# A decoder trunk with paged stick-breaking attention: where the sums of output-weight quarters are made, and where the convolution's first block and the lead pieces stand

## The chip, the core and the metric

The kernel runs on one NeuronCore of a Trainium2 chip, in one launch. Its engines are TensorE (PE, with its weight loads PEld), VectorE (DVE), ScalarE (ACT), GpSimd (POOL) and SyncE (SP); each works through its own row of instructions in order, and they meet through semaphores. Here SP issues nearly all plain DMA transfers, POOL the indirect ones (gathers). The metric is the device time of one execution in microseconds (us); smaller is better.

## The reference, cut to what matters

One decoder layer (`D_MODEL` 1024, mixer width 2048) runs for a prompt of 2048 tokens and for a sample group of 8 sequences with 4 tokens each and 8192 cached tokens in pages of 128:

```
h = rms_norm(x, pre_g)
z = h @ w_in                                   # 5632 columns, split into groups
A: u = a * sigmoid(b); causal depthwise conv, width 31; layer_norm; silu; @ w_pw + b_pw
B: causal means over windows of 2, 4, 8, 16, minus the token; per-group linear; scale
C: stick-breaking attention, 8 heads of 64:
   z = q.k/8 + bias;  a = exp(log_sigmoid(z) + sum over later keys of log_sigmoid(-z));  y = a @ v
D: cross-attention, 4 heads of 128, into 256 memory tokens
mix = concat(yA*silu(gA), yB*silu(gB), yC*silu(gC), yD*silu(gD))
y = x + rms_norm(mix @ w_out, post_g);  then a final rms_norm
```

The sample group's attention reads keys and values through a page table. All is fp32; the outputs are both groups' `y`, the new keys and values, the convolution and pooling states, and the prompt's memory keys and values.

## The kernel before, in words

**Projection.** `main` (L1927) runs `z_groups`, which multiply the normalised tokens by `w_in`. Each fp32 operand is split into a high part, rounded to the fast fp32r type, and a low part (a subtraction on DVE or POOL), and three matmuls take the place of one. Beside them live `tasks`: generators, of which each gets one step per step of `main` (later statistics, bias rows, convolution and pooling of finished columns). In the same loop the sample group's attention is fed in: POOL gathers pages of keys (`kt`, 128x2048, 1 MB) and of values (`vt`, 128x1024, 512 KB; both L957), DVE transposes the keys (`T`, L990), PE makes scores (`sSA`, L1003) and the weighted values (`sO`, L1042). The gathers are issued when the buffers that they fill come free, that is when DVE has transposed the keys before (`kt`) or PE has used the values before (`vt`).

**Prompt attention.** `sb_prompt` walks over four pairs of heads `hp` (called laps below), in each over four blocks of 512 queries `qb`, and in each over the key blocks `kc` from `qb` down to 0, with four score steps for each (`q2` 0 and 2, `hh` 0 and 1). Names like `be1_2_0_1_0` carry `hp`, `qb`, `kc`, `hh`, `q2`. One step is a chain over the engines: PE scores `S` (L1297, L1298), ACT sigmoids `gam` and `be` (L1302, L1303), a DVE scan `E` (L1372, L1375), a POOL product `be*E` (L1384), PE transposes `AT` (L1403), an ACT copy `at` (L1405), PE values `av` (L1415). At the end of a block DVE multiplies `av` by the gate rows `sgt` (L1419), in place, SP stores the result to `mixd` (L1420), and the next block's `sgt` is loaded (L1436) into the same single buffer. PE's row is laid out by hand, several steps deep; for the other engines a scheduler sets the order from the program and the pools' buffers, except where the program ties an instruction to another (`issue_after`, `keep_in_program_order`).

**Side work.** From the ninth step on, every time that 4.0 us of cost have gathered (`PACE`), the attention takes one step of `side_work` (L1990): the end of the sample group (`sample_end`), then `weight_sums`, then the first output weights (`out_weights(1)`: a load, an ACT cast `wohi` and a POOL subtraction `wolo`, eight times), then, once the block (3, 0) of the last lap is flagged, four *lead* pieces of `mix` (load `mr` L1731, ACT cast `mh` L1756, POOL subtraction), and after the flag (3, 1) three more loads and the start of the convolution's last part, `conv_post`, up to its flag `"centered"`. That start is: load two blocks of 256 tokens (`cy0`, `cy256`); add the four channel tiles of the first on POOL (`total`, `cs`, L1483); multiply by ones on PE for the mean (`center`, `cm0`, L1488); subtract on DVE; squares on ACT (`csq`, L1497); three additions of squares on POOL (L1499). The column sums of the second block (`cs256`) reuse the buffer of the first.

**Output.** `mix @ w_out` is done with seven products of quarter matrices instead of eight. Products 4 to 7 multiply *sums* of weight quarters with sums of mix quarters; products 1 to 3 use quarters as they are (`FACTORS`). `SUMS` names the place of each weight sum in the DRAM buffer `wsd`; `weight_load` reads it from there during the output stage. `weight_sums` (L1613) makes them in eight rounds: two loads of 512 KB each into SBUF (`ws`, L1620), four POOL operations on 128x512 (L1627), each tied behind the newest `be*E` product, and two stores of 512 KB to `wsd` (L1630). The mix sums are combined in `out_combine` (L1736) and the products' results in `out_ready` (L1773), with signs that belong to the signs of the weight sums.

Line numbers here and in the profile are those of the kernel before. In the changed kernel the attention's lines stand four further on (L1384 is L1388, L1420 is L1424, L1483 is L1487).

Of the kernel before, what the change touches and what calls it, by code (L numbers as in the profile page):

```python
# [18 lines left out]
P = 128  # L19
# [46 lines left out]
SUM = 3  # L66
BEB = 5
# [25 lines left out]
def kernel(  # L93
# [777 lines left out]

    def sample_setup(sm, S):
# [738 lines left out]
    SUMS = {4: (0, 0), 7: (0, 1), 6: (1, 0), 5: (1, 1)}  # L1611

    def weight_sums(wsp):  # L1613

        ts = {}
        for j in range(9):
            if j < 8:
                ts[j] = [wsp.tile([P, 2, 512], F32, tag="ws", name=f"ws{j}_{n}", bufs=6) for n in range(2)]
                for t, r in zip(ts[j], half_rows(j)[::-1]):
                    sp.dma_start(t.rearrange("p b n -> p (b n)"), w_out0[r])  # L1620
            yield
            if j:
                t, u = ts.pop(j - 1)
                for o, a, b, op_ in ((t[:, 1], t[:, 1], u[:, 1], ALU.subtract), (u[:, 1], u[:, 1], u[:, 0], ALU.subtract),
                                     (u[:, 0], t[:, 1], u[:, 0], ALU.add), (t[:, 0], t[:, 0], u[:, 0], ALU.subtract)):
                    with tc.issue_after(newest[-1]):
                        pool.tensor_tensor(out=o, in0=a, in1=b, op=op_)  # L1627
                    yield
                for n, o in enumerate((t, u)):
                    sp.dma_start(wsd[n, j - 1], o)  # L1630
                yield
# [104 lines left out]
    def out_combine(x):  # L1736
        prod, i, h = x
        store()
        ts = raws[x]
        if prod == 5 and i < LAST:  # L1740
            dve.tensor_tensor(out=ts[1], in0=ts[0], in1=ts[1], op=ALU.add)
            ts = ts[1:]
        elif prod == 7:
            pool.tensor_tensor(out=ts[0], in0=ts[0], in1=ts[1], op=ALU.subtract)
            stores.append(((0, i, h), msd[0, i, h], ts[0]))
        elif prod == 6:
            tc.keep_in_program_order(dve.tensor_tensor(out=ts[0], in0=ts[0], in1=ts[1], op=ALU.subtract))
# [25 lines left out]
    def out_ready(prod, i, o):  # L1773

        if i == LAST:
# [12 lines left out]
            else:  # L1788
                dve.tensor_tensor(out=o[:NS], in0=both[:NS], in1=keep["s"][:NS], op=ALU.add)
# [11 lines left out]
        elif prod == 6:  # L1801
            dve.tensor_tensor(out=U3[:, i], in0=o, in1=U3[:, i], op=ALU.add)
            dve.tensor_tensor(out=U2[:, i], in0=o, in1=U2[:, i], op=ALU.add)
# [5 lines left out]
        else:  # L1809
# [9 lines left out]
            dve.tensor_tensor(out=c, in0=o, in1=(U2 if prod == 3 else U3)[:, i], op=ALU.add)  # L1819
# [106 lines left out]

    def main():  # L1927
        yield from z_groups(0, GROUPS[0][4:12])
        tasks.add(later_stats())
        tasks.add(bias_rows())  # L1930
# [59 lines left out]
    def side_work():  # L1990
# [6 lines left out]
        yield from out_weights(1, opm, pool)  # L1997
        while (3, 0) not in flags:
# [15 lines left out]
        while "centered" not in flags:  # L2014
            next(conv)
            yield

# [195 lines left out]
```

## Time and profile before

| what | value |
|---|---|
| median of 3 runs | 2319.89 us (2316.73 to 2320.56) |
| the profiled execution | 2319.3 us, its span 2317.6 us |
| granted TensorE clock, mean over the span | 0.993 |
| busy: PE, PEld, DVE, ACT, POOL | 97%, 78%, 74%, 47%, 54% of the span |
| projection and sample group | 60 to 1465 us |
| prompt attention with side work | 1465 to 1902.4 us |
| output projection | 1902.4 to 2317.6 us |
| POOL operations of the weight sums (L1627) | 32, from 1550.0 to 1763 us |
| DMA | 558.32 MB, mean 241 GB/s |

How to read it: the profile is one execution, and all its times are microseconds from the start of the span. A busy share is an average over the stages, so what matters is read by stage: a window gives the busy time of each engine in a stretch, its granted PE clock (1.00 is full), the busy share of the 16 DMA engines and the rate. In a timeline a row gives start, length, engine, line, operation, and in brackets how long the engine stood idle before it and what it waited for. "SPq" is SP's row of DMA issues; a DMA's own time isn't in it.

### The profile page before, as it was taken

How to read it: one execution, taken by the hardware profiler on the slowest of the kernel's cores; microseconds unless marked ns; L12 is line 12 of the kernel's file. 1: busy time of each engine (PE TensorE's matmuls, PEld its weight loads, DVE VectorE, ACT ScalarE, POOL GpSimd, SP SyncE). 2: the span in 40 equal slices, each digit the busy share in tenths (PEclk: the TensorE clock that was granted, in tenths of full speed). 3: DMA queues.
4: the chain of work that ended last, by engine and by line, in shares of the span. 5: the costliest groups of instructions: out<-in, count | busy, mean ns of one | idle time of the engine just before them, and what ended most of it. 6: DMA issues, size and time to landing. Idle time of an engine off the chain costs nothing. (4 is left out here: it accounts for less than half of the span.)

```text
span 2317.6 us, 43407 instructions
## 1 busy us (share of the span) xinstructions
PE 2244.9 (97%) x16512; PEld 1812.9 (78%) x16512; DVE 1704.7 (74%) x2334; ACT 1081.0 (47%) x1977; POOL 1261.0 (54%) x1375
## 2 busy tenths in 40 slices
PE   7999999999999999999999999999999999999997
PEld 7998888898888777777777777667677667788775
DVE  5343786969756755378777768899989885686997
ACT  5332343242442322234233234588879875454553
POOL 3554545556464555555545455489999973620002
PEclk9999999999999999999999999999999999999999
DMA  6689977878778899987977885666554307876774
GB/s 206 208 291 316 336 259 255 286 256 277 255 252 301 306 358 338 345 284 255 319 260 259 278 275 178 160 173 192 160 161 129 98 15 217 285 236 194 251 261 152
DMA packets 338188, 558.32 MB, mean 241 GB/s; under 512 B 29162, under 2 KB 213610, under 8 KB 321580
## 3 DMA queue, kind: packets, MB, share of 16 engines
q1 hardware_dynamic: 282604, 286.83, 39.9%
q0 software_dynamic: 55376, 268.72, 32.8%
q8 instruction: 130, 2.13, 0.4%
q14 instruction: 78, 0.64, 0.1%
HBM read 465.35 MB, written 90.72 MB: 240 GB/s over the span
## 5 line engine op out<-in xcount | busy, mean ns | idle before, releaser
L990 DVE STREAM_TRANSPOSE T<-kt 128x1024 f32<-128x1024 f32 x256 | 308.6, 1226 | 183.1 <-PE sSA L1003 174.8
L957 POOL DMA_INDIRECT vt<-in_cache_v_dram,idv x256 | 252.7, 987 | 255.1 <-PE sO L1042 194.2
L642 DVE SCALAR_TENSOR_TENSOR cacc<-U,par,cacc 128x512 f32<-128x512 f32 x480 | 359.9, 750 | 11.0
L1384 POOL TENSOR_TENSOR be<-be,E 128x512 f32<-128x512 f32 (+4 forms) x316 | 311.9, 999 | 18.0 <-DVE E L1375 12.4
L957 POOL DMA_INDIRECT kt<-in_cache_k_dram,idk x128 | 128.7, 1005 | 200.2 <-DVE T L990 156.0
L1375 DVE TENSOR_TENSOR_SCAN E<-gam,cr,ZM 128x513 f32<-128x513 f32 x192 | 230.6, 1260 | 3.7 <-POOL csq L1499 1.0
L2032 PE MATMUL acc<-wohi,mh 128*128 128x512 f32 (+1 forms) x480 | 192.4, 401 | 0.0
L2032 PE MATMUL acc<-wolo,mh 128*128 128x512 f32 (+1 forms) x480 | 188.7, 393 | 0.0
L2032 PE MATMUL acc<-wohi,ml 128*128 128x512 f32 x448 | 176.9, 395 | 4.7 <-DVE ml L1767 4.7
L1405 ACT COPY at<-AT 128x512 f32<-128x512 f32 (+1 forms) x288 | 153.5, 592 | 47.9 <-PE AT L1403 42.9
L1403 PE MATMUL AT<-ident,be 128*128 128x128 f32 x1082 | 153.3, 281 | 14.6 <-ACT at L1405 10.9
L1403 PEld LDWEIGHTS AT<-ident,be 128*128 128x128 f32 x1082 | 121.2, 143 | 55.0 <-issue 22.8
L1303 ACT ACTIVATE be<-S 128x1024 f32<-128x1024 f32 (+1 forms) x158 | 153.8, 974 | 6.7 <-PE S L1298 4.1
L1415 PE MATMUL av<-at,V 128*64 128x256 f32 (+1 forms) x1152 | 137.4, 379 | 4.2 <-DVE sgt L1419 4.2
L1003 PE MATMUL sSA<-T,W 128*32 128x128 f32 x4096 | 138.3, 276 | 2.0 <-DVE T L990 1.6
L1297 PE MATMUL S<-kh,Q 128*128 128x512 f32 (+1 forms) x316 | 133.4, 426 | 1.5 <-ACT be L1303 1.5
L1003 PEld LDWEIGHTS sSA<-T,W 128*32 128x32 f32 x4096 | 104.6, 109 | 36.9 <-issue 29.0
L1415 PEld LDWEIGHTS av<-at,V 128*64 128x64 f32 x1152 | 76.6, 138 | 61.6 <-issue 23.3
L1042 PE MATMUL sO<-vt,saT 128*32 128x512 f32 x1024 | 122.4, 592 | 0.0
L1298 PE MATMUL S<-kl,Q 66*128 66x512 f32 (+1 forms) x316 | 119.5, 382 | 0.0
L1756 ACT CAST mh<-mr 128x512 fp32r<-128x512 f32 (+1 forms) x120 | 70.5, 596 | 96.5 <-PE acc L2032 26.8
L1767 DVE TENSOR_TENSOR ml<-mr,mh 128x512 fp32r<-128x512 f32 x108 | 80.6, 758 | 40.3 <-ACT mh L1756 40.0
(594 smaller groups left out, 6198.1 us busy)
## 6 DMA issues: line engine op xcount, KB each, us to landing
mr<-mixd SPq DMA_DIRECT2D x32, 512.0 KB
Q<-qd SPq DMA_DIRECT2D x96, 128.0 KB
mr<-mixd SPq DMA_DIRECT2D x48, 256.0 KB
xtp<-in_x_prompt_dram SPq DMA_DIRECT2D x16, 512.0 KB
kh<-kd SPq DMA_DIRECT2D x64, 128.0 KB
ws<-in_w_out_dram SPq DMA_DIRECT2D x16, 512.0 KB
wsd<-ws SPq DMA_DIRECT2D x16, 512.0 KB
msd<-mr SPq DMA_DIRECT2D x32, 256.0 KB
```

The lines of the kernel that those rows point to most:

```text
L642: dve.scalar_tensor_tensor(out=ps, in0=U[:, a + k : a + k + H], scalar=wd[:, k : k + 1], in1=ps, op0=ALU.mult, op1=ALU.add)
L957: pool.indirect_dma_start(out=dst, out_offset=None, in_=rows, in_offset=bass.IndirectOffsetOnAxis(ap=idx, axis=0))
L990: S["turn"] = dve.transpose(T[:, 2 * hh : 2 * hh + 2].rearrange("p s j t -> p (s j t)"), kt[:, 2 * hh : 2 * hh + 2].rearrange("p s j d -> ...
L1003: pe.matmul(sSs[n][32 * g : 32 * g + 32, P * ml : P * (ml + 1)], lhsT=W[:, jj, :], rhs=T[:, :, jj, :], start=i == 0, stop=i == 3, tile_pos ...
L1297: pe.matmul(S[:, j, :w], lhsT=Q[:, 0, c], rhs=kts[0][:, :w], start=True, stop=False)
L1303: act.activation(out=be, in_=S[:, :, :w], func=AF.Sigmoid)
L1375: dve.tensor_tensor_scan(out=E[:, j][:, ::-1], data0=g_[:, j][:, ::-1], data1=ZM[:, 0:1].to_broadcast([P, 513]), initial=carry[hh, q2][:, ...
L1384: newest.append(pool.tensor_tensor(out=be[:, j, :m], in0=be[:, j, :m], in1=E[:, j, 513 - w : 513 - w + m], op=ALU.mult).ins)
L1403: pe.transpose(ap_[:, n : n + P], A[hp, qb, kc, hh, qt][:, P * r : P * (r + 1)], ident)
L1405: act.copy(at[:, :n], ap_[:, :n])
L1415: pe.matmul(av[64 * hh : 64 * hh + 64, c], lhsT=V[:, 4 * kc + r, 64 * hh : 64 * hh + 64], rhs=ats.pop((hp, qb, kc, hh, q2, r)), start=dg a ...
L2032: pe.matmul(o[:rows], lhsT=m[a][:, k, :rows], rhs=W[prod, 4 * h + k][w], start=not cont and h == k == n == 0, stop=h == 1 and k == 3 and n ...
```

## The change

The weight sums leave the attention. `weight_sums` becomes a task of the projection, added in `main` after the first eight groups. It uses no SBUF and no arithmetic of an engine: SP copies 512 KB of a weight quarter from `w_out` to `wsd`, DRAM to DRAM, and four rounds later POOL issues a transfer of 512 KB that adds another quarter, or a sum made before, onto it. There are 16 copies and 16 such adds, in the order of the products 7, 5, 6, 4. Every copy is tied behind the newest instruction of SP, every add behind the newest of POOL, so that they keep their places in those rows; between a copy and an add lie six task steps, and six more before the next copy. The signs of the sums change, so signs change in `out_combine` and `out_ready` too; the count of operations there stays.

In `side_work` the SBUF pool of the sums is gone, `out_weights(1)` follows `sample_end` at once, and the start of `conv_post` comes next, ahead of the wait for the flag (3, 0). Then come the lead pieces, with the load of the next piece issued ahead of the work on one, and after the flag (3, 1) the three loads.

```
-    def weight_sums(wsp):
-
-        ts = {}
-        for j in range(9):
-            if j < 8:
-                ts[j] = [wsp.tile([P, 2, 512], F32, tag="ws", name=f"ws{j}_{n}", bufs=6) for n in range(2)]
-                for t, r in zip(ts[j], half_rows(j)[::-1]):
-                    sp.dma_start(t.rearrange("p b n -> p (b n)"), w_out0[r])
-            yield
...
+    def weight_sums():
+
+        def half(j, h):
+            k = 4 + j if j < 4 else j - 4
+            return [w_out0[P * r : P * (r + 2), 512 * h : 512 * h + 512].rearrange("(j p) n -> j p n", p=P)
+                    for r in (8 + j, k)]
+
+        def sums(prod, j):
+            n, h = SUMS[prod]
+            return wsd[n, j : j + 2, :, h]
+
+        def copy(prod, j):
+            u, t = half(j, 0 if prod in (4, 5) else 1)
+            with tc.issue_after(newest_on(mybir.EngineType.SP)):
+                sp.dma_start(sums(prod, j), u if prod == 5 else t)
+
+        def add(prod, j):
+            of = half(j, 1)[0] if prod in (5, 7) else sums(5 if prod == 6 else 6, j)
+            with tc.issue_after(newest_on(mybir.EngineType.Pool)):
+                pool.dma_start(out=sums(prod, j), in_=of, accum_op=ALU.add)
+
+        todo = [(prod, j) for prod in (7, 5, 6, 4) for j in range(0, 8, 2)]
+        for n in range(len(todo) + 4):
+            if n < len(todo):
+                copy(*todo[n])
+            for _ in range(SUMSTEP):
+                yield
+            if n > 3:
+                add(*todo[n - 4])
+            for _ in range(SUMSTEP):
+                yield
...
         yield from z_groups(0, GROUPS[0][4:12])
         tasks.add(later_stats())
+        tasks.add(weight_sums())
         tasks.add(bias_rows())
...
-        with tc.tile_pool(name="wsp", bufs=1, side="left", reuse_waits="tile") as wsp:
-            yield from weight_sums(wsp)
         opm = ox.enter_context(tc.tile_pool(name="opm", bufs=1, side="left", reuse_waits="tile"))
         yield from out_weights(1, opm, pool)
-        while (3, 0) not in flags:
-            yield
-        for x in lead_:
-            out_load(x)
-            out_combine(x)
-            out_high(x)
-            out_low(x, pool)
-            yield
-
-        while (3, 1) not in flags:
-            yield
-        for x in parts[2 * LEAD : 2 * LEAD + 3]:
-            out_load(x)
         cp = cx.enter_context(tc.tile_pool(name="cp", bufs=1, side="left", reuse_waits="tile"))
...
         while "centered" not in flags:
             next(conv)
             yield
+        while (3, 0) not in flags:
+            yield
+        out_load(lead_[0])
+        yield
+        for n, x in enumerate(lead_):
+            if n + 1 < len(lead_):
+                out_load(lead_[n + 1])
+            out_combine(x)
+            out_high(x)
+            out_low(x, pool)
+            yield
+        while (3, 1) not in flags:
+            yield
+        for x in parts[2 * LEAD : 2 * LEAD + 3]:
+            out_load(x)
+        yield
```

PE's row stays as it was but for the one matmul of `center` (`cm0`), which moves from the fourth lap to the second, into the block (2, 0). Rows of SP, POOL and ACT move.

SP's row at the start of the third lap, before (`kl3_0_1` are keys for the last lap, `ws5` a weight sum in SBUF, `sgt1_3` the last block of the second lap, `sgt2_0` the gate rows of the next):

```order
L1278 DMA kl3_0_1_18396<-kd_58 64x512
L1630 DMA wsd_71<-ws5_1_17253 128x1024
L1420 DMA mixd_63<-sgt1_3_17047 128x4x128
L1280 DMA kl3_0_1_18396<-bd_69 2x512
L1290 DMA V3_18406<-vd_59 128x16x128
L1436 DMA sgt2_0_17594<-gsd_61 128x512
L1630 DMA wsd_71<-ws5_0_17252 128x1024
```

And now:

```order
L1282 DMA kl3_0_1_18431<-kd_58 64x512
L1284 DMA kl3_0_1_18431<-bd_69 2x512
L1294 DMA V3_18441<-vd_59 128x16x128
L1424 DMA mixd_63<-sgt1_3_17117 128x4x128
L1440 DMA sgt2_0_17646<-gsd_61 128x512
```

The two stores of weight sums are gone, one of which stood ahead of the `mixd` store; the store and the load of the gate rows now stand behind the keys and values.

POOL's row in the second lap's block 2, before, where the column sums of the convolution's first block stand between two products:

```order
L1384 TENSOR_TENSOR be1_2_2_1_2_16738<-be1_2_2_1_2_16738,E1_2_2_1_2_16802 128x511
L1483 TENSOR_TENSOR cs0_19952<-cy0_19612 128x256
L1483 TENSOR_TENSOR cs0_19952<-cs0_19952,cy0_19612 128x256 x2
L1384 TENSOR_TENSOR be1_2_1_0_0_16775<-be1_2_1_0_0_16775,E1_2_1_0_0_16834 128x512
L1380 COPY cr1_2_1_0_0_16837<-E1_2_1_0_0_16834 128x2
```

In the same block of the same lap now (`cs256` belongs to the second block of tokens, `csq0` to the squares of the first):

```order
L1388 TENSOR_TENSOR be1_2_0_1_0_16981<-be1_2_0_1_0_16981,E1_2_0_1_0_17066 128x512 x2
L1487 TENSOR_TENSOR cs256_20539<-cy256_16311 128x256
L1503 TENSOR_TENSOR csq0_0_16996<-csq0_0_16996,csq0_1_16999 128x256
L1487 TENSOR_TENSOR cs256_20539<-cs256_20539,cy256_16311 128x256
L1503 TENSOR_TENSOR csq0_2_17002<-csq0_2_17002,csq0_3_17005 128x256
...
L1503 TENSOR_TENSOR csq0_0_16996<-csq0_0_16996,csq0_2_17002 128x256
L1388 TENSOR_TENSOR be1_2_0_0_2_17037<-be1_2_0_0_2_17037,E1_2_0_0_2_17127 128x512 x2
```

The sums of the first block have moved to the first lap's block (3, 3); in their lap stand the squares of the first block and the sums of the second, which stood together in the last lap's block 3.

POOL's row in the projection, at one of the accumulating transfers, before (gathers of keys and values, and the low part of a weight):

```order
L957 DMA kt36_0_9134<-in_cache_k_dram,idk_1378 128x2048
L957 DMA kt36_1_9220<-in_cache_k_dram,idk_1378 128x2048
L242 TENSOR_TENSOR wlo1v3_9236<-wr1v3_8977,whi1v3_9237 128x1024
L957 DMA vt35_0_9296<-in_cache_v_dram,idv_1379 128x1024
L957 DMA vt35_1_9298<-in_cache_v_dram,idv_1379 128x1024
```

And now:

```order
L961 DMA kt36_0_9163<-in_cache_k_dram,idk_1378 128x2048
L1932 DMA wsd_71<-wsd_71 256x512
L961 DMA kt36_1_9250<-in_cache_k_dram,idk_1378 128x2048
L243 TENSOR_TENSOR wlo1v3_9266<-wr1v3_9006,whi1v3_9267 128x1024
L961 DMA vt35_0_9326<-in_cache_v_dram,idv_1379 128x1024
```

The transfer stands in the row between two gathers of keys; around it the order is the same here.

ACT's row in the last lap at the first lead piece, before (`mh1_0_0` and `mh1_0_1` are the casts, `at3_1_0` copies of the lap's block 1, `be` and `gam` sigmoids of block 2):

```order
L1303 ACTIVATE be3_2_2_0_0_19411<-S3_2_2_0_0_19406 128x2x256
L1756 CAST mh1_0_0_19328<-mr1_0_0_19326 128x512
L1405 COPY at3_1_0_0_0_0_19421<-AT3_1_0_0_0_0_19420 128x512
L1756 CAST mh1_0_1_19378<-mr1_0_1_19376 128x512
L1405 COPY at3_1_0_0_0_1_19428<-AT3_1_0_0_0_1_19427 128x512
L1302 ACTIVATE gam2_14905<-S3_2_2_1_0_19434 128x2x256
```

And now:

```order
L1307 ACTIVATE be3_2_2_0_0_19385<-S3_2_2_0_0_19380 128x2x256
L1409 COPY at3_1_0_0_0_0_19395<-AT3_1_0_0_0_0_19394 128x512
L1739 CAST mh1_0_0_19352<-mr1_0_0_19304 128x512
L1409 COPY at3_1_0_0_0_1_19402<-AT3_1_0_0_0_1_19401 128x512
L1306 ACTIVATE gam2_14937<-S3_2_2_1_0_19408 128x2x256
```

The first cast stands one copy later, the second (`mh1_0_1`) six rows later and so not among these. The eight casts `wohi1` of the first output weights, which stood at the start of the last lap, stand from the first lap's block (3, 2) to the second lap's start.

More of the change, by code (lines that the diff above doesn't have):

```diff
@@ L66 @@
 SUM = 3
+SUMSTEP = 6
 BEB = 5
@@ L870, with newest_on @@
     sx = ExitStack()
+    def newest_on(eng):
+        return next(i for i in reversed(nc.cur_bb.bb.instructions) if i.engine == eng)
     def sample_setup(sm, S):
@@ L1610 @@
     FACTORS = {1: 11, 2: 21, 3: 22}
-    SUMS = {4: (0, 0), 7: (0, 1), 6: (1, 0), 5: (1, 1)}
-    def weight_sums(wsp):
-        ts = {}
-        for j in range(9):
-            if j < 8:
-                ts[j] = [wsp.tile([P, 2, 512], F32, tag="ws", name=f"ws{j}_{n}", bufs=6) for n in range(2)]
-                for t, r in zip(ts[j], half_rows(j)[::-1]):
-                    sp.dma_start(t.rearrange("p b n -> p (b n)"), w_out0[r])
-            yield
[L1622 to L1627, printed above, removed]
-                    yield
-                for n, o in enumerate((t, u)):
-                    sp.dma_start(wsd[n, j - 1], o)
-                yield
     def weight_load(prod, j, raw):
@@ L1740, in out_combine @@
         if prod == 5 and i < LAST:
-            dve.tensor_tensor(out=ts[1], in0=ts[0], in1=ts[1], op=ALU.add)
+            dve.tensor_tensor(out=ts[1], in0=ts[1], in1=ts[0], op=ALU.subtract)
             ts = ts[1:]
@@ L1746, in out_combine @@
         elif prod == 6:
-            tc.keep_in_program_order(dve.tensor_tensor(out=ts[0], in0=ts[0], in1=ts[1], op=ALU.subtract))
+            tc.keep_in_program_order(dve.tensor_tensor(out=ts[0], in0=ts[0], in1=ts[1], op=ALU.add))
             dve.tensor_tensor(out=ts[2], in0=ts[2], in1=ts[0], op=ALU.subtract)
@@ L1788, in out_ready @@
             else:
-                dve.tensor_tensor(out=o[:NS], in0=both[:NS], in1=keep["s"][:NS], op=ALU.add)
+                dve.tensor_tensor(out=o[:NS], in0=both[:NS], in1=keep["s"][:NS], op=ALU.subtract)
                 square(o, 16, 1)
@@ L1801, in out_ready @@
         elif prod == 6:
-            dve.tensor_tensor(out=U3[:, i], in0=o, in1=U3[:, i], op=ALU.add)
-            dve.tensor_tensor(out=U2[:, i], in0=o, in1=U2[:, i], op=ALU.add)
+            dve.tensor_tensor(out=U3[:, i], in0=U3[:, i], in1=o, op=ALU.subtract)
+            dve.tensor_tensor(out=U2[:, i], in0=o, in1=U2[:, i], op=ALU.subtract)
         elif prod == 2:
@@ L1818, in out_ready @@
                     g[0] = op.tile([P, 2, 512], F32, tag="raw", name=f"og{t}_0", bufs=RAWS)[:, 0]
-            dve.tensor_tensor(out=c, in0=o, in1=(U2 if prod == 3 else U3)[:, i], op=ALU.add)
+            dve.tensor_tensor(out=c, in0=o, in1=(U2 if prod == 3 else U3)[:, i],
+                              op=ALU.subtract if prod == 5 else ALU.add)
             square(c, t, half)
@@ L1925 @@
     sample = sample_all()
+    SUMS = {4: (0, 0), 7: (0, 1), 6: (1, 0), 5: (1, 1)}
+    def weight_sums():
[24 more added lines that the diff above has]
+                yield
     def main():
@@ L1993, in side_work @@
             yield from sample_end(sm2, side_ps, S)
-        with tc.tile_pool(name="wsp", bufs=1, side="left", reuse_waits="tile") as wsp:
-            yield from weight_sums(wsp)
         opm = ox.enter_context(tc.tile_pool(name="opm", bufs=1, side="left", reuse_waits="tile"))
         yield from out_weights(1, opm, pool)
+        cp = cx.enter_context(tc.tile_pool(name="cp", bufs=1, side="left", reuse_waits="tile"))
+        conv = conv_post(cp, lambda n: conv_ps[0](n), lambda: cx.enter_context(
+            tc.tile_pool(name="cpw", bufs=1, side="left", reuse_waits="tile")))
+        while "centered" not in flags:
+            next(conv)
+            yield
         while (3, 0) not in flags:
             yield
-        for x in lead_:
-            out_load(x)
+        out_load(lead_[0])
[3 more added lines that the diff above has]
+                out_load(lead_[n + 1])
             out_combine(x)
@@ L2010, in side_work @@
             out_load(x)
-        cp = cx.enter_context(tc.tile_pool(name="cp", bufs=1, side="left", reuse_waits="tile"))
-        conv = conv_post(cp, lambda n: conv_ps[0](n), lambda: cx.enter_context(
-            tc.tile_pool(name="cpw", bufs=1, side="left", reuse_waits="tile")))
-        while "centered" not in flags:
-            next(conv)
-            yield
+        yield
     def out_part(x):
```

## The prediction

> **What bounds the kernel now.** I read the page first, then the busy time by stage, the waits of PE in each stage, and the timelines around its waits. The page's first line gives the span. Below it are the three stages by windows (columns: stretch, length, then busy time and instructions of PE, PEld, DVE, ACT and POOL, granted clock, DMA share, GB/s).
>
> ```profile
> span 2317.6 us, 43407 instructions
> 60.00:1465.00 1405.00, 1392.10 (x11451) 1145.56 (x11450) 953.12 (x1324) 468.79 (x876) 756.83 (x700) 1.00 0.82 279
> 1465.00:1902.40 437.40, 414.32 (x2880) 303.76 (x2879) 401.33 (x414) 366.08 (x570) 395.52 (x542) 0.98 0.50 139
> 1902.40:2317.60 415.20, 390.53 (x1897) 318.49 (x1895) 317.36 (x546) 210.53 (x462) 87.69 (x87) 0.99 0.69 223
> ```
>
> PE is the bound everywhere. In the projection it idles 12.9 of 1405 us (1405.00 - 1392.10), at full clock. In the attention it idles 23.1 of 437.4, at 0.98. So a change that takes no matmul away can gain little in the first stage, and in the attention at most its idle time plus the lost clock. The attention's four laps, one per pair of heads, show where that lies:
>
> ```profile
> 1473.50:1577.72 104.22, 96.30 (x671) 69.90 (x669) 95.45 (x105) 86.97 (x136) 86.65 (x131) 0.97 0.64 176
> 1577.72:1683.49 105.77, 102.20 (x723) 74.62 (x722) 99.61 (x98) 89.83 (x139) 102.32 (x138) 0.98 0.61 176
> 1683.49:1790.35 106.86, 103.26 (x723) 75.98 (x722) 98.58 (x100) 91.36 (x142) 103.60 (x137) 0.97 0.50 141
> 1790.35:1902.40 112.05, 104.06 (x733) 76.22 (x732) 100.70 (x105) 96.82 (x155) 102.96 (x139) 0.98 0.24 66
> ```
>
> I call them laps 0 to 3. Laps 1 to 3 idle 3.57, 3.60 and 7.99 us, 15.2 in all, and their clock loses about 0.02, 0.03 and 0.02 of them, 7.6 more: 23 us is all that this part of the change can win. POOL is busy 97% of laps 1 and 2, and 83% of lap 0.
>
> **The weight sums leave the attention.** Here is the group of their Pool additions, and the same score steps in lap 2, with sums, and in lap 3, without:
>
> ```profile
> L1627 POOL TENSOR_TENSOR ws<-ws,ws x24: 1266/1280/1740, 1550.0 to 1762.5; 128x512 f32<-128x512 f32 x24
> 1741.83:1772.69 30.86, 30.76 (x224) 22.52 (x222) 28.80 (x30) 27.54 (x43) 30.37 (x40) 1.00 0.48 136
> 1849.48:1880.34 30.86, 30.76 (x224) 22.50 (x221) 28.32 (x30) 27.56 (x43) 25.89 (x37) 1.00 0.06 18
> ```
>
> All 32 additions (these 24 and 8 of the other form) at 1.28 us are 41 us of POOL. Yet the two stretches take 30.86 us each: PE runs full beside them, so the sums by themselves cost nothing. They cost only where something queues behind them. The first place is SP's row at the start of lap 2. The rows are SP, DVE, PE there, the same PE step in lap 1, and the window:
>
> ```profile
> 1697.59 0.61 SPq L1278 DMA_DIRECT2D kl<-kd  x1
> 1703.01 0.34 SPq L1630 DMA_DIRECT2D wsd<-ws  x1
> 1703.46 0.39 SPq L1420 DMA_DIRECT2D mixd<-sgt  x1
> 1707.12 0.47 SPq L1436 DMA_DIRECT2D sgt<-gsd  x1
> 1712.04 0.69 DVE L1419 TENSOR_TENSOR sgt<-av,sgt 128x512 f32<-128x512 f32 x1 [1.65 <-DMA sgt<-gsd]
> 1712.78 1.55 PE L1415 MATMUL av<-at,V 128*64 128x256 f32 x8 [2.83 <-DVE sgt L1419]
> 1708.76 0.48 PE L1297 MATMUL S<-kh,Q 128*128 128x512 f32 x1
> 1715.67 0.56 PE L1297 MATMUL S<-kh,Q 128*128 128x256 f32 x1
> 1602.73 0.48 PE L1297 MATMUL S<-kh,Q 128*128 128x512 f32 x1
> 1605.39 0.37 PE L1297 MATMUL S<-kh,Q 128*128 128x256 f32 x1
> 1708.00:1720.00 12.00, 9.17 (x53) 7.41 (x53) 10.25 (x12) 8.00 (x15) 10.26 (x11) 0.72 0.73 211
> ```
>
> SP stands 4.8 us (1698.20 to 1703.01) on a store of sums that POOL hasn't finished. Behind it stand the mixd store and then the load of the next gate rows, which needs the stored tile back. DVE multiplies late, and PE waits 2.83 us. The step takes 6.91 us where lap 1 has 2.66: 4.25, and the window's clock of 0.72 reaches beyond it. Ends: 1.65, since that is all that DVE itself waited, and 6.2 (idle 2.83 and 0.28 of 12). I take **-4.5**, nearest to the step's own row.
>
> [...]
>
> The second place is a burst of the convolution's column sums on POOL (its first block) in lap 1 (POOL, then PE, then the window):
>
> ```profile
> 1624.55 1.88 POOL L1483 TENSOR_TENSOR cs<-cs,cy 128x256 f32<-128x256 f32 x2
> 1626.39 1.08 POOL L1384 TENSOR_TENSOR be<-be,E 128x512 f32<-128x512 f32 x1
> 1627.53 0.33 PE L1403 MATMUL AT<-ident,be 128*128 128x128 f32 x1 [1.12 <-POOL be L1384]
> 1625.00:1635.50 10.50, 8.53 (x49) 5.80 (x48) 10.10 (x9) 7.56 (x11) 10.42 (x15) 0.84 0.63 211
> ```
>
> PE idles 1.97 us and loses 0.16 of 10.5 in clock: 3.65. The order moves this burst, so **-3.65** (ends 2.0 and 3.65). The burst that now stands in lap 0 meets a POOL with 17% free: **+0.5** (ends 0 and 3.65). Beyond these two places laps 1 and 2 idle 1.60 and 0.77 us, in gaps that end on POOL or ACT. With POOL 41 us lighter I take **-1.5** (ends 0 and -2.4).
>
> **Convolution's first block and lead.** These are the window of the lap's tail, then ACT, PE and the window at the lead:
>
> ```profile
> 1887.00:1902.40 15.40, 12.63 (x90) 9.07 (x89) 14.02 (x14) 12.38 (x22) 14.36 (x17) 1.00 0.01 2
> 1824.50 0.62 ACT L1756 CAST mh<-mr 128x512 fp32r<-128x512 f32 x1 [3.77 <-DMA mr<-mixd]
> 1825.75 0.63 PE L1403 MATMUL AT<-ident,be 128*128 128x128 f32 x4 [3.03 <-ACT at L1405]
> 1820.00:1833.00 13.00, 9.18 (x58) 6.96 (x58) 8.76 (x11) 8.06 (x15) 11.25 (x18) 0.87 0.55 147
> ```
>
> Lap 3's excess is 7.99 idle and about 2.2 of clock. The lead accounts for 5.5 (3.82 idle, 0.13 of 13). The tail, where the first block's center stands now, has 2.77 of idle in its window, and what is left of the excess is 4.7; I take 4.7. That leaves. But the center, its squares, their three POOL sums and the second block's three column sums arrive in lap 1, in one run of Pool's row between two products that PE waits for. There the same chain (matmul, DVE, ACT, POOL) must be gone through with be products queued behind it: 2 if the lighter POOL hides most, 7 if POOL and the clock add up. I take the same 4.7, so the move is worth **0** (ends -3 and +4).
>
> The lead pieces' cast held ACT 3.77 us for a load whose rows are stored only after the block ends. The loads still come after that store, and in ACT's row the first cast stands one place later only, behind one copy of at. So most of it stays: **-1.5** (ends 0 and -4; the second piece's load comes one piece ahead).
>
> The first weights' eight ACT casts move from lap 3 to the end of lap 0. First a window from there, then their row:
>
> ```profile
> 1553.60:1563.80 10.20, 10.10 (x73) 7.41 (x71) 10.10 (x10) 10.20 (x16) 10.20 (x12) 1.00 0.52 147
> L1663 ACT CAST wohi<-wor x8: 631/647/689, 1777.8 to 1812.4; 128x512 fp32r<-128x512 f32 x8
> ```
>
> ACT has nothing free in that stretch, and it makes the at tiles that PE waits for. Eight casts of 0.65 are 5.2 us, of which the buffers between the engines should hide more than half: **+1.5** net of the 0.5 that lap 3 gains (ends -0.5 and +4).
>
> Attention: -4.5 - 3.65 + 0.5 - 1.5 + 0 - 1.5 + 1.5 = **-9.15**.
>
> **What the projection gets.** 16 copies of 512 KB stand in SP's row at places that ran at 227 to 730 us, 16 accumulating transfers in POOL's row at 312 to 950, six of them after 730. The windows, the median landing of the gathers there (last column, us), PE's costliest wait of the stage, the one wait of a transpose for a gather, and the only plain transfer that POOL issues now:
>
> ```profile
> 220.00:730.00 510.00, 503.31 (x4500) 446.69 (x4500) 366.82 (x519) 183.18 (x352) 283.30 (x269) 1.00 0.80 276
> 730.00:960.00 230.00, 228.67 (x1842) 176.14 (x1841) 145.15 (x181) 65.58 (x120) 129.30 (x119) 1.00 0.96 335
> kt<-in_cache_k_dram,idk POOLq DMA_INDIRECT x74, 8.1
> vt<-in_cache_v_dram,idv POOLq DMA_INDIRECT x147, 6.3
> PE sSA L1003 <- DVE T L990: 1.6, 2, 1.4
>   DMA kt<-in_cache_k_dram,idk: 3.8, 1
> L1420 POOL DMA_DIRECT2D mixd<-sgt x1: 879/879/879, 1922.6 to 1922.6; - x1
> ```
>
> PE waits 1.6 us for transposes in the whole stage, so the gathers keep ahead now. On POOL an add costs about 0.9 us of issue, 14 in all, beside 648 us that POOL idles in this stage: nothing, unless it waits for its copy, four rounds older. In the engines' time, 512 KB at 335 GB/s is 1.6 us. The copies (25 us) find 102 us free before 730. No row shows an add. It passes at least 1.6 us of data and, if it reads both sides and writes one, 4.7; the step from the 512 KB gather to the 1 MB one (6.3 to 8.1) gives 1.8. I take 2.7. Six of them after 730 are 16 us where 0.04 of 230, 9 us, is free. The 7 us left over delay gathers, which have some room, as the one wait above shows. I take **+2** (ends -2, since the rows around are reshuffled and PE's 12.9 idle us could shrink, and +19, below).
>
> [...]
>
> **Output.** The order of PE and the sums read there stay: 0, with 1.5 either way.
>
> **Sum.** -9.15 + 2 + 0 = -7.15. The profiled run took 2319.3 us (span 2317.6 and 1.7 around it), 0.6 below the median of the three: 2319.9 - 7.15 = **2312.7**.
>
> **Rivals.**
> *The adds hold the gathers: slower.* Place: 730 to 960, where the DMA share is 0.96. If an add takes 4.7 us and a gather has 1.5 us of room (my estimate from the 1.6 us that PE waits now), six adds cost 6 x 3.2 = 19, net +10: **2330**. It decides from 3.8 us an add on (13.75 us more to end 4.6 slower, 2.3 for each of six, above the 1.5). For it: the share. Against it: PE's single small wait, and a DVE that mostly waits for PE.
> *The stalls only move: no change.* The lead's cast waits as before (0), the center costs 7 in lap 1 (+2.3), the casts 4, the burst in lap 0 3.65: -4.5 - 3.65 + 3.65 - 1.5 + 2.3 + 4 + 2 = +2.3, **2322**. It is the case where the change doesn't do what its words say, since a lead that comes later doesn't wait less.
> *Nearly all of it goes: faster by more.* POOL, 41 us lighter, takes the bursts in stride: -6.2 - 3.65 - 2.4 - 4.7 (the tail, with nothing in lap 1) - 1.5 + 0.5 is -18, **2302**. For it: POOL at 97% in laps 1 and 2 now. Against: the window in lap 2 that runs full beside the sums.
>
> **How the numbers follow.** What a measurement of this kernel can tell from no change is about 0.2%, 4.6 us. Chances: forecast 0.45, all goes 0.15, stalls only move 0.22, adds hold 0.18. So faster by over 0.2% 0.60 (the first two), within 0.2% 0.22, slower 0.18. The range reaches from the third rival's 2302 to just short of the first's 2330, **2301 to 2328**; the forecast's own is 2305 to 2318.
>
> **What would show it.** Right: lap 2's step at the sgt load takes 2.7 us, no Pool burst between 1623 and 1627 of lap 1's place, lap 3's tail without csq, lap 1 longer at the center, and transposes that wait for gathers under 5 us in all. Wrong: PE waits for T adding up to 10 us or more after 730; a lap 3 lead without a wait on ACT (then nearer 2308); laps 0 and 1 longer by more than the 7 us of center and casts.

## The result, and the profile after

The changed kernel takes **2417.20 us** (median of 6 runs, 2406.42 to 2421.34) against 2320.22 for the kernel before (6 runs, 2316.73 to 2326.01): a ratio of 1.0409, interval 1.0385 to 1.0434. It is 97 us slower, where 7 us faster was forecast and 2328 was the upper end of the range.

These are the page's lines on the span, on the engines and on the DMA queue that holds gathers and adds, of the kernel after and then of the kernel before (queue, kind: packets, MB, share of 16 engines' span):

```profile
span 2417.0 us, 43333 instructions
PE 2270.5 (94%) x16512; PEld 1831.6 (76%) x16512; DVE 1703.7 (70%) x2334; ACT 1073.6 (44%) x1973; POOL 1228.7 (51%) x1359
q0 software_dynamic: 59728, 277.11, 33.2%
```
```profile
q0 software_dynamic: 55376, 268.72, 32.8%
```

Busy time by stage of the kernel after, with the columns of the prediction's windows (projection, attention, output):

```profile
60.00:1569.80 1509.80, 1419.67 (x11448) 1166.99 (x11447) 960.43 (x1324) 462.51 (x871) 768.14 (x716) 0.97 0.81 271
1569.80:2002.60 432.80, 413.18 (x2880) 302.38 (x2878) 394.00 (x414) 365.26 (x570) 355.36 (x510) 0.98 0.39 101
2002.60:2417.00 414.40, 389.65 (x1896) 317.34 (x1894) 316.61 (x546) 210.25 (x462) 84.14 (x87) 0.99 0.69 224
```

The whole loss lies in the first stage: 1509.80 us against 1405.00, 104.8 longer. The attention is 4.6 shorter and the output 0.8 shorter. In the projection PE does the same matmuls (11448 against 11451 recorded). Its idle time grew from 12.9 to 90.1 us, and its busy time by 27.6, at a granted clock of 0.97 against 1.00: the longest gap, below, costs its own 16.9 us and then slower matmuls, with a granted clock of 0.50 over the next 5 us. The DMA share is 0.81 against 0.82, but of a longer stage, so the 16 engines were busy some 70 us more in it. The share alone tells nothing for or against the transfers.

PE's costliest waits in that stage, after (engine, line, what was waited for: us in total, times, longest):

```profile
PE xpsp L224 <- DVE xtp L216: 17.2, 2, 16.9
PE sSA L1007 <- DVE T L994: 15.9, 7, 6.5
PE py L622 <- DMA plw<-in_pool_w_dram: 11.8, 1, 11.8
PE nt1v L380 <- ACT zt1v L729: 9.7, 1, 9.7
PE z0mg L252 <- DVE sg0pg L735: 8.5, 2, 4.3
```

Before, the largest of them is the 1.6 us that the prediction quotes. The five are 63 of the 90 us, and they name five different tiles and three releasers. No single resource stands behind them, so each has to be followed up. The longest, 16.9 us, in the rows of DVE, POOL, SP and PE:

```profile
827.74 7.87 DVE L643 SCALAR_TENSOR_TENSOR cacc<-U,par,cacc 128x512 f32<-128x512 f32 x10
835.52 2.37 DVE L994 STREAM_TRANSPOSE T<-kt 128x1024 f32<-128x1024 f32 x2
837.81 0.42 DVE L743 TENSOR_TENSOR sg0cg<-z0cg,sg0cg 128x288 f32<-128x288 f32 x1
838.51 6.34 DVE L216 SCALAR_TENSOR_TENSOR xtp<-xtp,rs,gpre 128x1024 f32<-128x1024 f32 x1
839.12 4.65 POOL L243 TENSOR_TENSOR wlo1k<-wr1k,whi1k 128x1024 fp32r<-128x1024 f32 x2
820.53 0.69 SPq L355 DMA_DIRECT2D xtp<-in_x_prompt_dram  x1
845.00 1.09 PE L224 MATMUL xpsp<-ident,xtp 128*128 128x128 f32 x4 [16.93 <-DVE xtp L216]
```

Read it from the bottom. PE stands 16.93 us for a tile of normalised tokens `xtp`. Its load was issued at 820.53 and had landed by 828.1, so the data were there. What is late is the operation that normalises it, at 838.51 in DVE's row: ahead of it stand ten convolution accumulations in one run (7.87 us), transposes and gates, in all 20 accumulations since the tile before. Then it takes 6.34 us, where in the kernel before each of its kind takes 1.24 to 1.29. Two subtractions on POOL run beside it until 843.77; whether they hold it, no run here shows. None of the operations that PE waits behind is a copy or an add. In the kernel before, only three accumulations stand between the same two tiles:

```profile
749.57 0.74 DVE L642 SCALAR_TENSOR_TENSOR cacc<-U,par,cacc 128x512 f32<-128x512 f32 x1
750.83 1.53 DVE L642 SCALAR_TENSOR_TENSOR cacc<-U,par,cacc 128x512 f32<-128x512 f32 x2
756.20 2.46 DVE L215 SCALAR_TENSOR_TENSOR xtp<-xtp,rs,gpre 128x1024 f32<-128x1024 f32 x2
```

Behind the gap the clock is down. This is the window of the next 5 us in the kernel after, in the columns of the stages above, with a granted clock of 0.50; in the 10 us after it, it is 0.99:

```profile
845.00:850.00 5.00, 5.00 (x14) 4.13 (x15) 1.98 (x2) 0.59 (x1) 0.01 (x1) 0.50 1.09 314
```

Other waits have the same shape. The pooling weights `plw` stand 21 rows later in SP's row, copies not counted, and PE waits 11.8 us for them. The transposes `T` stand behind accumulations. The cast of the weights `whi0cg` stands 8 rows later in ACT's row; here it is before and after:

```profile
251.51 1.05 ACT L241 CAST whi0cg<-wr0cg 128x1024 fp32r<-128x1024 f32 x1 [1.47 <-issue]
```
```profile
268.67 0.39 ACT L1036 COPY saT<-sSA 128x256 f32<-128x256 f32 x1
268.94 1.07 ACT L242 CAST whi0cg<-wr0cg 128x1024 fp32r<-128x1024 f32 x1
```

Not all are of that shape: `zt1v` stands behind a cast that waits 14.46 us for a load of weights.

So a first theory: **rows**. With 32 transfers more in the program, the scheduler lays out the whole projection anew, and the waits come from that. By the names in the two traces, buffer numbers left out, at least some 35 instructions of ACT, 125 of DVE, 21 of POOL and 32 of SP have changed places. The rival: **traffic**. Copies and adds take time on the DMA engines and places in queues, and the waits come from late data, whatever the order.

### The profile page after: what moved, and what is told of

It reads as the page before. It is cut to its first block, busy times and chain, and to the rows that moved or that the text cites. A ratio compares the mean times of both kernels' runs of the same rounds, so it can differ in the third digit from the quotient of the medians.

```text
span 2417.0 us, 43333 instructions
## 1 busy us (share of the span) xinstructions
PE 2270.5 (94%) x16512; PEld 1831.6 (76%) x16512; DVE 1703.7 (70%) x2334; ACT 1073.6 (44%) x1973; POOL 1228.7 (51%) x1359
## 3 DMA queue, kind: packets, MB, share of 16 engines
q0 software_dynamic: 59728, 277.11, 33.2%
## 5 line engine op out<-in xcount | busy, mean ns | idle before, releaser
L1007 PE MATMUL sSA<-T,W 128*32 128x128 f32 x4096 | 143.1, 281 | 16.3 <-DVE T L994 15.9
L1419 PEld LDWEIGHTS av<-at,V 128*64 128x64 f32 x1152 | 76.6, 138 | 58.4 <-issue 25.5
```

What stands on the lines that cost most here:

```text
L1007: pe.matmul(sSs[n][32 * g : 32 * g + 32, P * ml : P * (ml + 1)], lhsT=W[:, jj, :], rhs=T[:, :, jj, :], start=i == 0, stop=i == 3, tile_pos ...
L1419: pe.matmul(av[64 * hh : 64 * hh + 64, c], lhsT=V[:, 4 * kc + r, 64 * hh : 64 * hh + 64], rhs=ats.pop((hp, qb, kc, hh, q2, r)), start=dg a ...
```

## The experiments

### Order and traffic taken apart

Two kernels cross the two theories. `rows_of_before` is the changed kernel, its copies and adds in their places, but every other instruction of ACT, DVE, POOL and SP in the projection is held in the order of the kernel before. `rows_of_after` is the reverse: the sums stay in the attention as before, nothing is copied or added in the projection, and the rows are held in the order of the changed kernel. Both have the new order of the side work. In their traces the four rows stand in the order that was asked for. The edit, where ROWS lists for each engine how far an instruction stands from its place in the program:

```
+    def tie_rows(skip):
+        for eng, text in ROWS.items():
...
+            row = [traced[n + d] for n, d in enumerate(steps)]
+            for a, b in zip(row, row[1:]):
+                tc.add_manual_dep(b, a.name, mybir.DependencyInfo(
+                    mybir.DependencyClass.NoSync, mybir.DependencyReason.DATA), reason="issue_after")
```

> The changed kernel, with all its copies and adds at their places, but the rows of ACT, DVE, POOL and SP in the projection tied to the order in which they stand in the kernel before. Theory R (rows): the 105 us of the projection were lost because the scheduler, which laid the rows by its own estimate of the transfers, put weight casts, transposes and loads later in those rows; the transfers themselves cost little. Then the projection comes back to within 10 us of before's and the time is 2310 to 2325 us. Theory T (traffic, the first rival of the prediction): copies and adds hold the DMA engines, loads and gathers land late. Then the time stays at 2400 to 2420 us. Half and half would be near 2365.

Measured: 2339.02 us (4 runs, 2335.57 to 2343.11), ratio 1.0099 (1.0068 to 1.0130). That is 14 us above the range of theory R and far from that of T.

> The reverse: no copies and no adds in the projection (the weight sums made in SBUF beside the attention, as before, with the side work in the changed order), but the rows of ACT, DVE, POOL and SP in the projection tied to the order in which they stand in the changed kernel. Theory R: the loss comes with the rows alone, 2400 to 2425 us. Theory T: without the traffic nothing is lost, 2312 to 2325 us.

Measured: 2398.07 us (4 runs, 2384.79 to 2402.11), ratio 1.0337 (1.0293 to 1.0382). That is 2 us below the range of theory R and far from that of T.

The projection in `rows_of_before`, and PE's waits there:

```profile
60.00:1490.90 1430.90, 1399.45 (x11450) 1148.53 (x11449) 954.64 (x1324) 468.61 (x875) 772.12 (x716) 0.99 0.84 286
PE nt1v L380 <- ACT zt1v L729: 8.4, 1, 8.4
PE smt L1208 <- DMA mkb<-in_cache_mem_k_dram: 3.9, 1, 3.9
PE sSA L1007 <- DVE T L994: 3.2, 3, 1.6
```

And in `rows_of_after`:

```profile
60.00:1543.70 1483.70, 1410.51 (x11444) 1158.89 (x11445) 958.73 (x1324) 462.95 (x871) 751.87 (x700) 0.98 0.78 264
PE xpsp L223 <- DVE xtp L215: 17.2, 2, 16.9
PE sSA L1003 <- DVE T L990: 13.3, 6, 6.5
PE py L621 <- DMA plw<-in_pool_w_dram: 7.1, 1, 7.1
```

| projection, us | order of before | order of after |
|---|---|---|
| no copies, no adds | 1405.0 | 1483.7 (+78.7) |
| copies and adds | 1430.9 (+25.9) | 1509.8 (+104.8) |

The two parts add up: 78.7 + 25.9 = 104.6. That they do so to 0.2 us is luck, since each figure is one profiled execution and the runs of `rows_of_after` alone spread over 17 us; by the medians of the whole time it is 78.1 + 19.1 = 97.2 against 97.0. The wait of 16.9 us for `xtp` comes with the order alone, where no byte is copied or added in that stage, and it is gone with the old order although all 32 transfers run. The transposes' waits follow the order too (13.3 us with it alone, 3.2 with the traffic alone). Rows are three quarters of the loss, traffic one quarter.

### The side work alone

`side_only` is the kernel before with only the new order of the convolution's first block and of the lead pieces; the sums are made in SBUF as before.

```
         yield from out_weights(1, opm, pool)
+        cp = ...
+        while "centered" not in flags:
+            next(conv)
+            yield
         while (3, 0) not in flags:
             yield
```

> The kernel before with only the second part of the change: the first weights, the start of the convolution and the lead pieces in their new order, the weight sums as before in SBUF. The projection's rows are those of before, so both theories expect the projection unchanged. By the prediction's terms (center moved 0, lead -1.5, casts +1.5, burst in the first lap +0.5, the late gate rows and POOL's load not gone) the time is 2318 to 2324 us; if the attention's gain of 5 us in the changed kernel came from this part, it is 2313 to 2316.

Measured: 2316.91 us (10 runs), ratio 0.9988 (0.9973 to 1.0004), between the two ranges expected. The interval takes in no change. Its profile has an attention of 431.2 us against 432.7, both counted from PE's first score to its first output product. This part of the change costs nothing that can be measured and brings at most a few microseconds.

### Which of the transfers

`copies_only` is the changed kernel with the adds left out, its rows as the scheduler lays them. `rows_copies` leaves the same adds out of `rows_of_before`.

```
-            if n > 3:
-                add(*todo[n - 4])
```

> The changed kernel without the 16 adds: the copies stay, so every sum lacks its second quarter. In its rows the cast of the seventh weight column and the load of the pooling weights still stand late. Theory R: most of the loss stays, 2380 to 2420 us. Theory T with the adds as the holders: the copies find free DMA time before 730 us, 2312 to 2335 us.

Measured: 2435.33 us (one run, before 2319.96). With half the transfers, this one run is slower than every run with all of them. Taking the adds out let the scheduler lay the rows anew once more (the wait for `xtp` grew to 19.0 us), so this run says nothing on the adds by themselves; it says that the order can be worth more than they are.

> Rows of before tied as in the first experiment, copies at their places, but no adds (each sum lacks its second quarter). It splits the 26 us that the projection still lost there. If the adds on the gathers' queue cost them (theory A), the projection is within 5 us of before's and the time 2312 to 2320 us; if the copies do (theory C), it stays at 2334 to 2342 us.

Measured: 2326.36 us (10 runs, 2322.66 to 2334.22), ratio 1.0029 (1.0014 to 1.0043). It lies between the two theories' ranges. Against `rows_of_before` the 16 adds cost 2339.02 - 2326.36 = 12.7 us by the medians and 16 by the ratios. Its profile gives less for them. Here is the projection:

```profile
60.00:1484.90 1424.90, 1399.23 (x11450) 1149.19 (x11450) 953.99 (x1324) 468.24 (x876) 755.50 (x700) 1.00 0.82 281
```

It is 6.0 us shorter than in `rows_of_before` and 19.9 longer than in the kernel before, but the profiled run, 2334.22, is the slowest of the ten. So of the 25.9 us the adds cost 6 to 16 and the copies the other 10 to 20. Both cost something; the split isn't settled.

What an add does to its surroundings shows in `rows_of_before`. First POOL, then ACT, then the window:

```profile
863.34 1.06 POOL L1934 DMA_DIRECT2D wsd<-wsd  x1
879.69 1.04 ACT L242 CAST whi1v<-wr1v 128x1024 fp32r<-128x1024 f32 x1 [13.23 <-DMA wr1v<-in_w_in_dram]
880.64 0.58 ACT L729 COPY zt1v<-z1v 128x512 f32<-128x512 f32 x1
859.00:880.00 21.00, 13.82 (x92) 10.87 (x90) 15.87 (x21) 2.07 (x4) 5.54 (x6) 0.89 1.03 327
```

And the cast in `rows_copies`, with the same rows and no add:

```profile
878.40 1.05 ACT L242 CAST whi1v<-wr1v 128x1024 fp32r<-128x1024 f32 x1 [3.20 <-PE z1v L252]
```

The 16 DMA engines are full there (1.03). The add goes in among the gathers and a load of weights, and the load is late: its last piece lands 20.5 us after the issue, and 8.6 us in `rows_copies`, where the same window has a share of 0.98. ACT stands 13.23 us at its cast, and behind the cast, in ACT's row, stands the copy of `zt1v` for which PE then waits 8.4 us. Without the add the cast waits for PE alone. The sufferer here is SP's load of weights, not the gathers: the transposes that wait for them stay at 3.2 us.

### Two engines' rows at a time

`rows_act_dve` holds only ACT and DVE in the order of before, `rows_sp_pool` only SP and POOL.

```
+            if eng not in (mybir.EngineType.Activation, mybir.EngineType.DVE):
+                continue
```

> The changed kernel with copies and adds, but only the rows of ACT and DVE in the projection tied to those of before; SP and POOL stand as the scheduler lays them. If the loss comes from casts and transposes that stand late on ACT and DVE, the time is near that of all four rows tied, 2335 to 2350 us; if from loads that stand late in SP's row (the pooling weights, the tokens' tiles) and products in POOL's, it stays above 2370 us.

Measured: 2380.87 us (4 runs), ratio 1.0258 (1.0231 to 1.0285). The projection is 66.5 us longer than before: of the 78.9 us that all four rows win back (104.8 - 25.9), these two win 38.3. By its time alone the run fits the second expectation, that loads in SP's row and products in POOL's carry the loss.

> The complement of the run with ACT and DVE tied: copies and adds in the projection, the rows of SP and POOL tied to those of before, ACT and DVE as the scheduler then lays them. ACT and DVE tied left 66 us of the projection's loss, all four tied 26, none 105. If the two halves add up, this run loses 26 + (105 - 66) = 65 us there, 2375 to 2385 us; if either half alone makes the loss (an instruction waits for the later of the two), it loses 26 to 40, 2335 to 2355 us.

Measured: 2416.64 us (4 runs), ratio 1.0413 (1.0388 to 1.0438): as slow as the change itself, with a projection 103.1 us longer than before. It fits neither expectation. PE's waits in its projection:

```profile
PE z0mg L252 <- DVE sg0pg L735: 20.1, 4, 9.8
PE xpsp L224 <- DVE xtp L216: 17.2, 2, 16.9
```

With SP and POOL held, the scheduler laid ACT and DVE out anew once more, in an order that is neither that of before nor that of the change, and the waits for `sg0pg` grew from 8.5 to 20.1. So the two runs give no share of the loss for each pair of engines, since the pair left free gets a new order each time. What they do show is where a single wait hangs. The 16.9 us at `xtp` stand as they were, since in DVE's row 20 accumulations stand ahead of the tile here too; in `rows_act_dve`, with DVE's row held, the longest wait for `xtp` is 2.3 us. So that wait hangs on DVE's row and not on SP's.

### The transfers put into the attention

If the projection is the wrong place, the attention has room by its windows: lap 3 before has a DMA share of 0.24, and after the change lap 2 has 0.37. Four kernels put the 32 transfers there, so that the projection has none of them. `att_sums_first` runs them after `sample_end`, `att_sums_beside` one with each step of the rest of the side work (its wrapper also drops the value that held some of those steps to every other attention step).

```
-        tasks.add(weight_sums())
...
         opm = ox.enter_context(tc.tile_pool(name="opm", bufs=1, side="left", reuse_waits="tile"))
+        yield from weight_sums()
         yield from out_weights(1, opm, pool)
```

> The changed kernel with the 16 copies and 16 adds taken out of the projection and put where the sums stood before, in the side work behind the sample group's end, one copy and one add by turns (one step apart). The projection's rows are then those of before. Theory R with its rest (rows cost 79 us, the traffic 26 us, both only because they meet the gathers and the loads of the projection): the projection is as long as before's and the attention 4 to 5 us shorter, 2312 to 2317 us. Rival: the adds hold POOL (1 us each to issue) and the DMA engines while the attention loads its keys and queries, and the time is 2320 us or more.

Measured: 2337.71 us (6 runs), ratio 1.0073 (1.0052 to 1.0094).

> The same, but the copies and adds run beside the rest of the side work, one step of them with each step of it, so that the first weights, the start of the convolution and the lead pieces keep the early places that they have in the changed kernel. Theory R: 2312 to 2317 us as well, its attention as long as the changed kernel's (428 us). The rival as in the run before: 2320 us or more.

Measured: 2356.72 us (5 runs), ratio 1.0161 (1.0136 to 1.0185).

The projections are back (1475.1 and 1471.6 us to the first score, against 1469.7), but the attentions take 451.6 and 470.8 against 432.7, counted as above. In `att_sums_beside` one wait alone is 25.5 us:

```profile
PE S L1301 <- DMA Q<-qd: 26.2, 2, 25.5
```

That could be rows again, so `att_sums_tied` holds all four engines, up to the end of the attention, to the order that they have with no transfer in the program. `att_sums_late` does so too and starts the transfers behind the convolution's first block, in laps 1 and 2, at half the rate.

```
         while "centered" not in flags:
             next(conv)
             yield
+        yield from weight_sums()
         while (3, 0) not in flags:
```

> The copies and adds beside the attention again (one step of them with each step of the other side work; all fall into the first two laps), but the rows of ACT, DVE, POOL and SP, from the kernel's start to the attention's end, are tied to the order that the scheduler gives the changed kernel when it has no copies and adds at all. If the 20 and 38 us that the two runs before lost in the attention came from rows laid anew (gate products late on DVE, loads late on SP), they go, and the time is 2310 to 2318 us: the projection as before, the attention 427 to 430. If the transfers themselves hold up POOL (1 us each to issue) and the loads of keys, queries and gates, the time stays at 2325 us or more.

Measured: 2336.49 us (7 runs), ratio 1.0062 (1.0040 to 1.0084).

> As in the run before with the sums beside the attention and the rows tied through the attention's end, but the 16 copies and 16 adds come later: behind the start of the convolution, so in the second and third lap, where the first weights' loads, casts and subtractions are over and the sample group's last work too. If the 16 us that the earlier places cost in the attention came from meeting that work on POOL and on SP's queue, the attention takes 426 to 430 us and the whole 2310 to 2316 us, 0.2 to 0.4% below the kernel before. If any place in the attention costs them (an add holds POOL, or the gates' and queries' loads wait for the copies), the time is 2322 us or more.

Measured: 2339.51 us (5 runs), ratio 1.0090 (1.0075 to 1.0106).

Neither became faster than before: their attentions take 448.7 and 450.9 us. With the rows held the loss stays, so a new order at each placing is not what costs here. The order that they are held to was not run without its transfers, so that it costs nothing by itself is assumed, not shown. `att_sums_late` at the start of lap 2, SP, then DVE, PE and the window:

```profile
1713.29 11.18 SPq L1424 DMA_DIRECT2D mixd<-sgt  x1
1724.52 2.76 SPq L1929 DMA_DIRECT2D wsd<-in_w_out_dram  x1
1730.48 0.34 SPq L1440 DMA_DIRECT2D sgt<-gsd  x1
1733.75 0.69 DVE L1423 TENSOR_TENSOR sgt<-av,sgt 128x512 f32<-128x512 f32 x1 [11.34 <-DMA sgt<-gsd]
1734.50 1.55 PE L1419 MATMUL av<-at,V 128*64 128x256 f32 x8 [13.76 <-DVE sgt L1423]
1705.00:1735.00 30.00, 16.24 (x115) 11.87 (x114) 17.93 (x20) 15.95 (x25) 18.22 (x28) 0.83 0.94 216
```

It is the chain of the prediction's first place, through the single buffer `sgt`: store to `mixd`, landing, load of the next gate rows, DVE, PE. The issue of the store alone takes 11.18 us, and PE stands 13.76. The engines are 0.94 busy at only 216 GB/s, where the projection's window before, as busy (0.96), moved 335. In `att_sums_tied` a late convolution load holds POOL, and with it the `be*E` products behind that sum:

```profile
1560.52 0.72 POOL L1487 TENSOR_TENSOR cs<-cy 128x256 f32<-128x256 f32 x1 [12.03 <-DMA cy<-ydw]
PE AT L1407 <- POOL be L1388: 8.5, 1, 8.5
```

A mean DMA share leaves out that the attention hangs on short transfers with nothing between them and PE: 13.76 us here through the load of `sgt`, 25.5 in `att_sums_beside` for that of `Q`.

## Why the prediction was wrong, point by point

**The projection, +2: the step that failed.** The prediction set the upper end of this stage at +19 and gave the reshuffled rows as a reason for a gain ("since the rows around are reshuffled and PE's 12.9 idle us could shrink"). It priced each add and copy as if all else stayed, and gave no price to a single moved row, though four engines' rows were moved all through the stage. They cost 78.7 us, as `rows_of_after` shows. The argument that PE "idles 12.9 of 1405 us" should have cut the other way: in a stage so tightly packed a new order has 13 us to win, and no row before gives a bound on what it can lose.

**The adds.** Taken at 2.7 us of the 16 engines, between 1.6 and 4.7. In the trace after an add is 256 packets of 2 KB, 16 for each of the 16 engines on average; a packet takes 176 to 243 ns in the mean of one add: 2.8 to 3.9 us. The queue's two lines above agree roughly: 33.2% of 2417.0 less 32.8% of 2317.6 is 42 us, 2.6 for each of 16. So size and bounds held. What failed is the cover: the "7 us left over" were to hide in the gathers' room. They cost 6 to 16 us; the one place followed up goes through a load of weights and the row behind it. The copies, costed at nothing in the 102 us that the engines have free before 730, cost 10 to 20.

**The first rival.** It was right in sign and wrong in place and size. Gathers were not held (T waits 3.2 us with the adds and the old order), and 2330 is 87 us short. The sign that was named for it, waits for T of 10 us or more after 730, did not appear: after 730 they are 1.4 us. The 15.9 us of the whole stage stand earlier, and 13.3 of such waits come with the new order and no add at all.

**An add from POOL's queue beside a load from SP's.** The load landed 20.5 us after its issue in `rows_of_before`, with the add, and 8.6 in `rows_copies`, without it. The prediction put up to 19 us on the adds in the projection; adds and copies together cost 25.9.

**The attention, -9.15: the sign right, the size too large.** Measured -4.6 in the change; the four kernels that differ from it only in the projection's rows and adds (`rows_of_before`, `rows_copies`, `rows_act_dve`, `rows_sp_pool`) have -5.4 to -8.2. By terms of the change, from the same score steps before and after:

| term | predicted | measured |
|---|---|---|
| lap 2, `sgt` load behind the store of sums | -4.5 | -4.7 (6.91 to 2.87, next 2.56 to 1.86) |
| lap 1, Pool burst of the first block | -3.65 | -3.7 |
| lap 0, that burst arrives | +0.5 | none seen |
| small gaps | -1.5 | -2.1 |
| center: lap 3's tail, its arrival in lap 1 | -4.7 and +4.7 | -3.5 and +6.05 |
| lead pieces | -1.5 | -1.8 |
| casts of the first output weights | +1.5 | about +6 |

Here are the tail, after, in a window of the same length, and the place of the casts at the start of lap 1 (ACT, then PE):

```profile
1987.20:2002.60 15.40, 15.02 (x113) 10.93 (x111) 15.05 (x14) 13.90 (x21) 12.58 (x15) 1.00 0.00 1
1685.12 0.64 ACT L1646 CAST wohi<-wor 128x512 fp32r<-128x512 f32 x1
1685.63 1.11 ACT L1409 COPY at<-AT 128x512 f32<-128x512 f32 x2
1691.88 1.06 PE L1407 MATMUL AT<-ident,be 128*128 128x128 f32 x8 [2.56 <-ACT at L1409]
```

PE's idle time in the tail's window fell from 2.77 to 0.38 us, but lap 3's last step is as long as it was (5.28 and 5.30 us): part of the excess that was called the center is the emptying of the lap, and it stays. The casts were the term most off. Buffers were to hide "more than half" of 5.2 us, and nothing was hidden. The table's terms sum to -3.75; the 0.85 that remain are not placed. That the loss at the casts comes from them rests on the rows' neighbourhood and on no run of its own; the eight POOL subtractions `wolo` moved there with them.

**Output, 0.** It is -0.8 in the windows, within the 1.5 that was given.

**What stays open.** Why the scheduler moves so many rows when transfers are added: its choice is made before the program runs, and no trace shows its reasons. What each moved row costs by itself: a kernel with some rows held gives the others yet another order. Why the late `xtp` operation itself takes 6.34 us. Whether some order of the rows makes the sums free: none of the versions run beat the kernel before, and `side_only` can't be told from it.

## What to carry to other kernels

Where a scheduler lays the rows, a transfer that is added has two prices, its traffic and the order of everything else (25.9 and 78.7 us of the projection here); compare the rows of every engine, and give the moved ones a term whose upper end is open wherever PE has nearly no idle time left. To learn which it is, hold the old order with the new work and the new order without it: here the two halves added up to 104.6 of 104.8 us, while removing half of the transfers with the order left free had only raised the time. A low mean DMA share (0.24 in lap 3 before, 0.37 in lap 2 after) was no room for bulk transfers here, where the work hangs on a store, its landing and the next load through one buffer: with them the attentions took 16 to 38 us longer.

## What the runs showed of the hardware

An accumulating transfer between two places in DRAM was dear: 176 to 243 ns for a packet of 2 KB, as means of the 16 adds in the kernel after. By that 512 KB take 2.8 to 3.9 us of all 16 engines, an estimate, against 1.6 us at the 335 GB/s that the projection before moved from 730 to 960 us. Some issues took long where the DMA engines were full. These are the issues of copies and adds in the kernel after (count: min/median/max in ns, first and last start in us):

```profile
L1927 SPq DMA_DIRECT2D wsd<-in_w_out_dram x16: 496/582/5917, 229.3 to 784.4; - x16
L1932 POOL DMA_DIRECT2D wsd<-in_w_out_dram x8: 976/1046/1312, 316.5 to 644.6; - x8
L1932 POOL DMA_DIRECT2D wsd<-wsd x8: 994/1042/1287, 724.1 to 1048.1; - x8
```

A copy's issue on SP, 0.58 us in the median of the 16, took 5.92 once, and the store to `mixd` in `att_sums_late` took 11.18; the DMA share over the two is 1.04 and 1.09. Behind that store SP's row has its next issue at 1724.52, 0.05 us after the store's ended. In the kernel after, POOL's issues stayed at 0.98 to 1.31 us.
